# Two of the first three loads issued by GpSimd behind its first mask instead of at once, in a kernel for the diagonal of a 2-D prefix sum

## Chip, cores and metric

The kernel runs on one core of one Trainium2 chip. The metric is the time of one execution on the device, in microseconds (us), as the median of several runs.

## The reference

```python
def setup_inputs():
    B, H, W = 4, 4224, 4224
    return {"x": np.random.randn(B, H, W).astype(np.float32)}

def reference(x):
    ps = np.cumsum(np.cumsum(x, axis=1), axis=2)
    diag = np.diagonal(ps, axis1=1, axis2=2)
    return np.cumsum(diag, axis=1).astype(np.float32)
```

Of each 4224 x 4224 prefix sum only the diagonal is wanted, and its running sum. The element at row i and column j enters every diagonal entry from max(i, j) on, so all of x, 285 MB, has to be read once.

## The kernel before

GpSimd loads strips of 768 rows (128 partitions x 6 rows) and converts float32 to bf16 on the way. TensorE adds up columns with a selector matrix; DVE multiplies the diagonal block with a triangular mask and sums rows; ScalarE sums other columns. Three strip buffers rotate, so the load of strip 3 waits until strip 0 has been used. A small "head" (0.54 MB of the last rows) comes through another queue, that of SyncE.

The opening, which the change touches:

```python
    NBUF = 3
    strips = ctx.enter_context(tc.tile_pool(name="strips", bufs=NBUF))
    # ...
    ctx.enter_context(tc.manual_schedule())      # program order is kept on each engine
    # ...
    nc.sync.dma_start(out=head, in_=src_a[:, :, N - HC : N])

    def strip_tile():
        return strips.tile([P, F2, N], BF16, name="strip")

    def load_rows(o, b, r0):
        f = o.shape[1]
        nc.gpsimd.dma_start(
            out=o, in_=x[b, r0 : r0 + f * P, :].rearrange("(p f) w -> p f w", f=f))

    prefetched = []
    for i in range(NBUF):                        # the three issues
        t = strip_tile()
        load_rows(t, 0, i * F2 * P)
        prefetched.append(t)

    hs = last.tile([P, 3], FP32, name="hs")
    nc.vector.reduce_sum(out=hs[:, 0:2], in_=head, axis=AX.X)   # DVE's first work: waits for the head
    # ... sel: small memsets on DVE

    def upper_mask(f):
        um = consts.tile([P, f, f * P], BF16, name=f"um{f}")
        nc.vector.memset(um, 1.0)
        nc.gpsimd.affine_select(out=um, in_=um, ...)            # waits for DVE's memset
        return um

    um6 = upper_mask(F2)
    um3 = upper_mask(F)
    # ... um1, ident, and some 20 small constants on GpSimd and DVE
```

And the main loop, which takes the strips:

```python
        for s in range(ns):
            strip = prefetched.pop(0) if prefetched else None
            if strip is None:
                strip = strip_tile()
                load_rows(strip, b, s * F2 * P)
            add_up(strip, F2, s * F2 * P, acc6[:, s], um6, by_rows=whole and s > 0)
            # ...
```

Of the kernel before, what the change touches and what calls it, by code (L numbers as in the profile page):

```python
# [17 lines left out]
def kernel(  # L18
# [18 lines left out]
    P = 128  # L37
    F = 3
    F2 = 2 * F
# [6 lines left out]
    NBUF = 3  # L46
# [24 lines left out]
# [6 lines that stand above are left out]
            out=o, in_=x[b, r0 : r0 + f * P, :].rearrange("(p f) w -> p f w", f=f)  # L77
        )

    prefetched = []  # L80
    for i in range(NBUF):
        t = strip_tile()
        load_rows(t, 0, i * F2 * P)
        prefetched.append(t)


    hs = last.tile([P, 3], FP32, name="hs")
# [6 lines left out]
# [4 lines that stand above are left out]
        nc.gpsimd.affine_select(  # L98
            out=um,
            in_=um,  # L100
            compare_op=ALU.is_gt,
            fill=0.0,
            base=0,
            pattern=[[-1, f], [1, f * P]],
            channel_multiplier=-f,
        )
        return um
# [2 lines left out]
    nc.vector.tensor_copy(out=sel_f, in_=sel)  # L110

    um6 = upper_mask(F2)
    um3 = upper_mask(F)
    um1 = consts.tile([P, GW], BF16, name="um1")
    nc.vector.memset(um1, 1.0)
# [484 lines left out]
```

## Time and profile before

| | before |
|---|---|
| time, median of the first 3 runs | 667.52 us (667.36 to 668.04) |
| span of the profiled run | 665.9 us |
| DMA queue of the strip loads | 142.47 MB written, 99.9% of the 16 engines' span |
| DVE, PE, ACT, GpSimd busy | 57%, 31%, 20%, 5% |

The busy shares say that no compute engine is the bound, and the line of DMA shares, nines in all slices but the last, that the loads are. Such a kernel is lost or won in two places only: at its two ends, and wherever the loads might run dry. The prediction shows and reads the lines.

One more view: the chain of work that ended last. In the kernel before, its first 60 us run from the issue of strip 0 straight to that strip's landing (columns: start us, us, what):

```profile
1.33 33.81 DMA strip<-in_x_dram
...
35.16 2.57 DVE mu L356
```

### The profile page before, as it was taken

The page shows a single profiled execution, that of the slowest core. Times are in us where ns is not written, and L with a number is a line of the kernel's source. Part 1 is how long each engine was busy: PE and PEld are TensorE (multiplying, and loading weights), DVE is VectorE, ACT ScalarE, POOL GpSimd, SP SyncE. Part 2 cuts the span into 40 slices and gives each one's busy share as a digit, 9 for nine tenths or more (in the row PEclk, how much of TensorE's full clock was granted, in tenths as well). Part 3 has the DMA queues.
Part 4 walks back from the last instruction along what each step waited for, and adds up shares of the span by engine and source line. Part 5 has one row for each costly group of instructions (what it writes and reads, how often), then busy time and mean ns, then how long its engine had stood idle before and what let it go on. Part 6 is the DMA issues. An engine that isn't in the chain of part 4 may idle for free.

```text
span 665.9 us, 2495 instructions
## 1 busy us (share of the span) xinstructions
PE 205.2 (31%) x948; PEld 94.0 (14%) x948; DVE 380.9 (57%) x176; ACT 136.1 (20%) x219; POOL 31.3 (5%) x59
## 2 busy tenths in 40 slices
PE   0070522302117143140311723404031354350428
PEld 0030211100003021010100311201000131120103
DVE  4160828476946183756794526456589434362866
ACT  0000121406300103040630020304063002030434
POOL 4200000000000000000000000000000000001000
PEclk9995857656558585665655857657565595775758
DMA  9999999999999999999999999999999999999998
GB/s 203 219 219 218 219 213 213 212 218 219 219 219 218 218 220 216 218 215 212 218 219 218 218 218 219 218 216 217 215 215 218 218 216 216 218 219 218 213 210 163
DMA packets 7650, 143.23 MB, mean 215 GB/s; under 512 B 682, under 2 KB 982, under 8 KB 2134
## 3 DMA queue, kind: packets, MB, share of 16 engines
q0 software_dynamic: 7296, 142.47, 99.9%
q1 hardware_dynamic: 342, 0.61, 0.3%
q8 instruction: 7, 0.11, 0.1%
q14 instruction: 5, 0.04, 0.0%
HBM read 285.47 MB, written 0.07 MB: 429 GB/s over the span
## 4 chain that ended last, share of the span: by engine, by line
DVE 51%; another core or an unknown queue 35%; DMA 12%; PE 1%; issue 1%; POOL 0%; DVEq 0%; POOLq 0%
DVE acc L261 27%; DMA strip<-in_x_dram 12%; DVE mu L356 7%; DVE strip L357 7%; DVE rowed L261 7%; PE d L214 1%; DVE c L487 0%; DVE whole_sums L487 0%; POOL strip L452 0%; DVE pu L261 0%; DVE whole_sums L282 0%; POOL strip L441 0%; DVE acc L381 0%; DVE rows L408 0%
## 5 line engine op out<-in xcount | busy, mean ns | idle before, releaser
L256 ACT ACTIVATE dump<-strip 128x416 bf16<-128x416 bf16 (+6 forms) x108 | 124.4, 1152 | 520.5 <-DMA strip<-in_x_dram 517.8
L356 DVE TENSOR_TENSOR mu<-strip,um 128x4608 bf16<-128x4608 bf16 (+1 forms) x24 | 52.4, 2183 | 256.9 <-DMA strip<-in_x_dram 256.8
L261 DVE TENSOR_REDUCE acc<-strip 128x6 f32<-128x4608 bf16 (+6 forms) x23 | 195.9, 8517 | 0.4
L221 PEld LDWEIGHTS <-sel 128*11 128x11 bf16 x643 | 66.6, 104 | 477.8 <-issue 448.1
L214 PE MATMUL d<-strip,sel 128*11 128x384 bf16 x90 | 37.1, 412 | 296.9 <-DMA strip<-in_x_dram 296.9
L221 PE MATMUL d<-strip,sel 128*11 128x384 bf16 x441 | 115.6, 406 | 0.0
L357 DVE TENSOR_TENSOR strip<-strip,mu 128x4608 bf16<-128x4608 bf16 (+1 forms) x24 | 52.4, 2183 | 1.0
L214 PE MATMUL d<-mu,sel 128*11 128x384 bf16 x43 | 16.3, 379 | 108.5 <-DVE mu L356 108.5
L261 DVE TENSOR_REDUCE rowed<-strip 128x384 f32<-128x2304 bf16 x12 | 48.9, 4079 | 0.0
L221 PE MATMUL d<-mu,sel 128*11 128x384 bf16 x200 | 46.3, 366 | 0.0
L76 POOL DMA_DIRECT2D strip<-in_x_dram x24 | 16.5, 687 | 537.9 <-DVE acc L261 292.7
L256 ACT ACTIVATION_READ_ACCUMULATOR dump<-strip 128x1 f32 x108 | 20.1, 186 | 0.0
L214 PE MATMUL d<-rowed,sel_f 128*11 128x384 f32 x24 | 11.7, 573 | 20.7 <-DVE rowed L261 20.7
L214 PEld LDWEIGHTS <-sel 128*11 128x11 bf16 x134 | 13.6, 102 | 24.1 <-issue 12.2
L214 PE MATMUL d<-ident,rows 128*11 128x128 f32 x24 | 5.2, 379 | 16.8 <-DVE rows L417 16.8
L261 DVE TENSOR_REDUCE pu<-d 11x1 f32<-11x384 f32 x4 | 2.2, 546 | 6.2 <-PE d L214 6.2
L97 DVE MEMSET um<- 128x4608 bf16 (+1 forms) x2 | 4.9, 2458 | 1.1 <-issue 1.1
L98 POOL TENSOR_SCALAR_AFFINE_SELECT um<-um 128x4608 bf16<-128x4608 bf16 (+1 forms) x2 | 5.2, 2610 | 7.5 <-DVE um L97 7.5
L214 PE MATMUL d<-halves,rows 128*11 128x64 f32 x48 | 5.3, 289 | 0.0
L214 PEld LDWEIGHTS d<-ident,rows 128*11 128x11 f32 x24 | 2.5, 119 | 18.9 <-DVE rows L417 11.7
L214 PEld LDWEIGHTS d<-rowed,sel_f 128*11 128x11 f32 x24 | 1.4, 92 | 25.3 <-DVE rowed L261 25.0
L214 PEld LDWEIGHTS d<-halves,rows 128*11 128x11 f32 x48 | 4.8, 129 | 1.3 <-issue 1.1
(105 smaller groups left out, 60.8 us busy)
## 6 DMA issues: line engine op xcount, KB each, us to landing
strip<-in_x_dram POOLq DMA_DIRECT2D x19, 6336.0 KB, 72.7
strip<-in_x_dram POOLq DMA_DIRECT2D x5, 3168.0 KB, 55.8
strip<-in_x_dram POOLq DMA_DIRECT2D x1, 1080.0 KB, 49.9
strip<-in_x_dram POOLq DMA_DIRECT2D x1, 768.0 KB, 52.9
strip<-in_x_dram POOLq DMA_DIRECT2D x3, 256.0 KB, 54.2
head<-in_x_dram SPq DMA_DIRECT2D x1, 528.0 KB, 3.7
strip<-in_x_dram POOLq DMA_DIRECT2D x1, 192.0 KB, 43.2
strip<-in_x_dram POOLq DMA_DIRECT2D x1, 64.0 KB, 28.7
```

Source lines behind the costliest of these rows:

```text
L76: nc.gpsimd.dma_start(out=o, in_=x[b, r0 : r0 + f * P, :].rearrange("(p f) w -> p f w", f=f))
L97: nc.vector.memset(um, 1.0)
L98: nc.gpsimd.affine_select(out=um, in_=um, compare_op=ALU.is_gt, fill=0.0, base=0, pattern=[[-1, f], [1, f * P]], channel_multiplier=-f,)
L214: nc.tensor.matmul(o, lhsT=lhsT, rhs=rhs, start=start, stop=False, skip_group_check=True)
L221: te.add_instruction(mybir.InstMatmult(start_tensor_calc=False, stop_tensor_calc=False, tile_position=(0, 0), tile_size=(P, P if lhsT.shap ...
L256: nc.scalar.activation(out=dump[:, :w], in_=src, func=ACT.Copy, accum_out=acc)
L261: nc.vector.reduce_sum(out=acc, in_=src, axis=AX.X)
L356: nc.vector.tensor_mul(out=mu, in0=block, in1=um)
L357: nc.vector.tensor_sub(out=block, in0=block, in1=mu)
```

## The change

GpSimd is to issue only strip 0 at once, then make its first mask, and issue strips 1 and 2 behind it. The intent that one can read from it: the first load should not share GpSimd with the two that are not needed yet, and since strip 0 takes 30 us to arrive, the others have time.

```diff
     prefetched = []
-    for i in range(NBUF):
+
+    def prefetch():
         t = strip_tile()
-        load_rows(t, 0, i * F2 * P)
+        load_rows(t, 0, len(prefetched) * F2 * P)
         prefetched.append(t)
+
+    prefetch()
@@
     um6 = upper_mask(F2)
+    for i in range(1, NBUF):
+        prefetch()
     um3 = upper_mask(F)
```

## The prediction

> **What bounds the kernel now.** I began with the page: the clock line, the line of DMA shares, the queues and the HBM traffic.
>
> ```profile
> PEclk9995857656558585665655857657565595775758
> DMA  9999999999999999999999999999999999999998
> GB/s 203 219 219 218 219 213 213 212 218 219 219 219 218 218 220 216 218 215 212 218 219 218 218 218 219 218 216 217 215 215 218 218 216 216 218 219 218 213 210 163
> ...
> q0 software_dynamic: 7296, 142.47, 99.9%
> ...
> HBM read 285.47 MB, written 0.07 MB: 429 GB/s over the span
> ```
>
> All forty slices but the last have the DMA engines at 90% or more, and one queue (q0, the loads that GpSimd issues) owns 99.9% of it. The busiest compute engine, DVE, has 57%. So the time is that of one stream: 142.47 MB written into SBUF, twice that read from HBM because the loads turn float32 into bf16. Then I read the end of the chain of work, from 600 us on:
>
> ```profile
> 607.31 11.72 another core or an unknown queue
> 619.03 0.28 issue
> 619.32 43.23 DMA strip<-in_x_dram
> ```
>
> The last load ends at 619.32 + 43.23 = 662.55 us; what follows is 665.9 - 662.55 = 3.35 us of tail. Last, the stretches and the timeline of the opening, where the change acts (a row of stretches gives the busy time of PE, PEld, DVE, ACT and POOL, each with its instructions, then clock, DMA share and GB/s):
>
> ```profile
> 1.00:2.00 1.00, 0.00 (x0) 0.00 (x0) 0.00 (x0) 1.00 (x1) 0.67 (x1) 1.00 0.07 11
> 2.00:3.00 1.00, 0.00 (x0) 0.00 (x0) 0.00 (x0) 0.09 (x1) 1.00 (x3) 1.00 0.79 167
> ...
> 60.00:630.00 570.00, 174.86 (x786) 80.06 (x786) 336.22 (x117) 122.50 (x198) 17.58 (x27) 0.63 1.01 217
> ```
>
> ```profile
> 1.33 2.27 POOL L76 DMA_DIRECT2D strip<-in_x_dram  x3 [0.81 <-POOLq L584]
> 4.59 1.25 DVE L88 TENSOR_REDUCE hs<-head 128x2 f32<-128x1056 f32 x1 [4.59 <-DMA head<-in_x_dram]
> 7.12 3.90 DVE L97 MEMSET um<- 128x4608 bf16 x1 [0.90 <-issue]
> 11.09 4.06 POOL L98 TENSOR_SCALAR_AFFINE_SELECT um<-um 128x4608 bf16<-128x4608 bf16 x1 [7.50 <-DVE um L97]
> 12.60 0.17 DVE L127 MEMSET ident<- 128x128 f32 x1
> 17.01 0.23 DVE L140 TENSOR_TENSOR halves<-ident 128x64 f32<-128x64 f32 x1 [4.24 <-POOL ident L128]
> 21.24 0.24 POOL L203 IOTA steps<- 128x128 int32 x1
> 35.16 2.56 DVE L356 TENSOR_TENSOR mu<-strip,um 128x4608 bf16<-128x4608 bf16 x1 [11.63 <-DMA strip<-in_x_dram]
> 46.45 0.78 POOL L76 DMA_DIRECT2D strip<-in_x_dram  x1 [24.97 <-PE d L221]
> 65.17 2.56 DVE L356 TENSOR_TENSOR mu<-strip,um 128x4608 bf16<-128x4608 bf16 x1 [19.87 <-DMA strip<-in_x_dram]
> ```
>
> The reader is to see four things. GpSimd issues three strips in 2.27 us. The small head load lands at 4.59 us and starts DVE, whose memset of the first mask (ends 11.02) releases GpSimd's select (ends 15.15). Strip 0 starts the real work at 35.16 and strip 1 at 65.17, 30.0 us apart. And between 15 and 35 us only setup runs.
>
> The floor: 142.47 MB at the 217 GB/s of the 60 to 630 us stretch is 656.5 us. Everything else in the span is 665.9 - 656.5 = 9.4 us: start, tail, small irregularities.
>
> **What the Trainium skill says.** "DMA: Bandwidth & Descriptors", Specifications, gives the DMA fabric a ceiling of 435 GB/s and HBM per core about 358. The trace reads 429 GB/s over the span, and 434 in the middle (2 x 217): the stream stands at the first ceiling, and above the second, so here the measurement decides against the 358. The same page, Queues, rings and completion order, says that an engine takes its ring's descriptors in order and switches between queues at packet boundaries. The trace agrees as far as it goes: strips land in the order of issue, 30.0 us apart, though three were queued at once. "Perfetto Trace Analysis", DMA Instruction — SWDGE, says that the record of such an issue ends with descriptor generation, not with the data: here 0.76 us per issue (2.27 / 3) against some 30 us of transfer. "SBUF — State Buffer", Who interferes with whom, says that DVE in a two-port mode can lock GpSimd out; the timeline has DVE idle from 12.77 to 17.01, just where the two moved issues would go, so I expect no such block.
>
> **The change part by part.** The order of instructions of both builds differs on GpSimd alone: DVE, PE, ACT and SP keep their sequence and what they wait for. No byte of traffic is added or removed.
>
> Taken away: two issues from about 2.1 to 3.6 us. Strip 0's own issue stays first at 1.33, so the stream's start stays. What might gain is the time until strip 0's first packet. The packet records have the first strip packet at about 3.7 us, 0.1 us after the third issue ends, so perhaps strip 0 becomes visible only when GpSimd is through with all three. But the head load has the engines until then: on 15 of 16 engines the first strip packet begins within some 0.02 us of the head's last record. Gain 0 to 0.7 us, of which I take 0.2.
>
> Added: the same two issues after the first mask. GpSimd waits for DVE's memset as before, ends the select at 15.15, and issues strips 1 and 2 from 15.2 to 16.7 (2 x 0.76 = 1.5 us). Are they in time? Strip 0 keeps all engines busy until just before 35.1. From an issue to its first packet I estimate 2.4 us (1.33 to 3.7, the head included), so strip 1 is ready at about 17.6 and strip 2 at 18.4, against 35.1: a reserve of 17 us. The engines never run dry, and strip 1 still lands at 65.1.
>
> Moved: all of GpSimd's later setup by 1.5 us. The identity ends at 18.5 instead of 17.0, the last iota at 23.0 instead of 21.5; DVE's setup ends at 25.0 instead of 23.5. DVE is next needed at 35.16, after an idle 11.63 us that falls to about 10.1. GpSimd's next issue, at 46.45, came after 24.97 us of waiting for PE; that becomes 23.4 and ends at the same moment.
>
> Sum on the path that sets the end: -0.2 (start) + 0 (strip 1 in time) + 0 (setup hidden) = -0.2 us. **667.52 - 0.2 = 667.3 us.**
>
> **The rivals.** First, starvation: if something holds the mask back, strips 1 and 2 wait behind it, since GpSimd works in order. The weak link is the head load, which DVE awaits first. If strip 0's packets, visible earlier, got between the head's, the head's 16 packets on an engine would each wait for a strip packet of 1.89 us (packet records), up to 30 us. The head at 27 us instead of 4.6 moves the mask's end from 15.2 to about 37.6 and strip 1's first packet to 40: 5 us of dry engines, 672.5 us; at the full 30 us delay some 12 us, 680 us. For it: the first strip packet follows the head so closely that nothing shows what happens when they meet. Against it: the head's packets start at about 1.9 us, before strip 0's issue has ended (2.1), and when strip packets appear the other engines finish their head first. I give this 4%.
>
> Second, the earlier start as a real gain: if strip 0's visibility was held back and the engines had time to spare, the whole stream moves forward by up to 1.5 us (the two issues): 666.0 us. The records of the head speak against more than half of it. One detail leaves a door open: the first strip packet lasted 3.11 us instead of 1.89, and one engine then finished strip 0 about 0.75 us behind the other 15. If that slow packet was an accident of three issues at once, its 0.75 us comes back: 666.8 us.
>
> Third, a shallower queue: for some 13 us only one strip is queued instead of three. If the engines needed more queued work for their rate, strip 0 would land later than 35.1. Nothing in the trace shows this state, but 16 packets per engine are queued in one strip. At a loss of 5% over 13 us it would be 0.65 us: 668.2 us.
>
> **Range and chances.** The three runs of before lie within 667.36 and 668.04, and another chip or session may shift that by 0.1 to 0.2%, or about 1 us. With gains of up to 1.5 us and small losses I set 665.8 to 669.0 us. Faster by over 2% means 13.4 us saved, more than the 9.4 us that exist beside the stream: practically excluded, 0.003. Slower by over 2% needs strip 1's first packet 13.4 us after 35.1, hence an issue no earlier than about 46 us: possible only with nearly the worst form of the first rival, 0.012.
>
> **What would show it.** In the changed kernel's timeline: the head's reduce still at 4.6 us, the select ending at 15.2, two issues at 15.2 to 16.7, DVE's setup ending at about 25.0, its first strip at 34.5 to 35.2 and the second 30.0 us later, GpSimd's fourth strip near 46.4 with a wait of about 23.4 us for PE, and the DMA line still all 9s. A second strip more than 30.5 us behind the first would prove starvation; a head after 5 us would name its cause; a first strip before 34.5 would prove the second rival. The prediction is wrong if the engines run dry at 35 us, or if the stream's rate in mid-kernel leaves 217 GB/s.

## The result, and the profile after

The changed kernel took 667.78 us (median of 6 runs, 667.38 to 669.75), the kernel before 667.75 us in its six runs (667.19 to 669.69). The ratio is 1.0001, with a 95% interval of 0.9983 to 1.0018: the same. (A ratio is the mean time of one kernel's runs over the mean time of the other's in the same rounds, so it is not quite the ratio of the medians.) Over all sessions the changed kernel had 17 runs with a mean of 668.53 us and the kernel before 43 runs with a mean of 668.56 us.

The timeline of the opening of the changed kernel (start us, us, engine, line, operation, names, shapes, and in brackets the idle time before it and what ended it):

```profile
1.33 0.82 POOL L76 DMA_DIRECT2D strip<-in_x_dram  x1 [0.81 <-POOLq L589]
...
4.56 1.25 DVE L91 TENSOR_REDUCE hs<-head 128x2 f32<-128x1056 f32 x1 [4.56 <-DMA head<-in_x_dram]
...
11.06 4.06 POOL L101 TENSOR_SCALAR_AFFINE_SELECT um<-um 128x4608 bf16<-128x4608 bf16 x1 [8.91 <-DVE um L100]
...
15.07 1.46 POOL L76 DMA_DIRECT2D strip<-in_x_dram  x2
...
18.43 0.23 DVE L145 TENSOR_TENSOR halves<-ident 128x64 f32<-128x64 f32 x1 [5.70 <-POOL ident L133]
...
22.67 0.24 POOL L208 IOTA steps<- 128x128 int32 x1
...
34.50 2.56 DVE L361 TENSOR_TENSOR mu<-strip,um 128x4608 bf16<-128x4608 bf16 x1 [9.55 <-DMA strip<-in_x_dram]
...
45.17 0.76 POOL L76 DMA_DIRECT2D strip<-in_x_dram  x1 [22.27 <-PE d L226]
...
64.48 2.56 DVE L361 TENSOR_TENSOR mu<-strip,um 128x4608 bf16<-128x4608 bf16 x1 [19.85 <-DMA strip<-in_x_dram]
```

The two issues now stand at 15.07. Everything that GpSimd does after them comes 1.4 us later (the identity's reader on DVE 18.43 instead of 17.01), and the waits shrink in exchange: DVE waited 9.55 us for strip 0 instead of 11.63, GpSimd 22.27 us for PE instead of 24.97. Strip 1 follows strip 0 by 64.48 - 34.50 = 29.98 us, as before (30.01).

The page of the changed kernel, its DMA shares and its HBM traffic:

```profile
DMA  9999999999999999999999999999999999999998
...
HBM read 285.47 MB, written 0.07 MB: 429 GB/s over the span
```

Same stream, same rate. Now the chain of work that ended last, in its first 60 us:

```profile
0.82 3.72 DMA head<-in_x_dram
...
7.08 3.91 DVE um L100
...
11.06 4.01 POOL um L101
15.07 49.32 DMA strip<-in_x_dram
```

This is a trap for the reader. The chain now leads through the head, DVE's memset and the mask to the issue of strip 1, as if the mask held up the kernel. But the 49.32 us of that step run from issue to landing, and the transfer itself takes 30. The remaining 19 us strip 1 lay queued behind strip 0. A chain that follows each wait back to its issue does not know of the queue; whether the issue is critical has to be asked of the chip, and the first experiments do that.

### The profile page after: what moved, and what is told of

The parts are those of the page before. It is cut to its first block, busy times and chain, and to the rows that moved or that the text cites. A ratio compares the mean times of both kernels' runs of the same rounds, so it can differ in the third digit from the quotient of the medians.

```text
span 665.7 us, 2495 instructions
## 1 busy us (share of the span) xinstructions
PE 201.5 (30%) x948; PEld 92.7 (14%) x948; DVE 380.9 (57%) x176; ACT 136.1 (20%) x219; POOL 31.3 (5%) x59
## 4 chain that ended last, share of the span: by engine, by line
DVE 50%; another core or an unknown queue 32%; DMA 14%; POOL 1%; issue 1%; PE 1%; DVEq 0%; POOLq 0%
DVE acc L266 26%; DMA strip<-in_x_dram 14%; DVE rowed L266 7%; DVE mu L361 7%; DVE strip L362 7%; PE d L219 1%; POOL um L101 1%; DVE um L100 1%; DMA head<-in_x_dram 1%; DVE c L492 0%; DVE whole_sums L492 0%; POOL strip L457 0%; DVE pu L266 0%; DVE whole_sums L287 0%
## 5 line engine op out<-in xcount | busy, mean ns | idle before, releaser
L226 PEld LDWEIGHTS <-sel 128*11 128x11 bf16 x643 | 65.4, 102 | 475.7 <-issue 444.7
L219 PE MATMUL d<-strip,sel 128*11 128x384 bf16 x90 | 36.5, 406 | 296.5 <-DMA strip<-in_x_dram 296.5
L226 PE MATMUL d<-strip,sel 128*11 128x384 bf16 x441 | 113.3, 399 | 0.0
L219 PEld LDWEIGHTS <-sel 128*11 128x11 bf16 x134 | 13.2, 99 | 24.6 <-issue 12.6
```

The costliest lines, as they stand in the source:

```text
L219: nc.tensor.matmul(o, lhsT=lhsT, rhs=rhs, start=start, stop=False, skip_group_check=True)
L226: te.add_instruction(mybir.InstMatmult(start_tensor_calc=False, stop_tensor_calc=False, tile_position=(0, 0), tile_size=(P, P if lhsT.shap ...
```

## The experiments

Ten runs were made: six edited kernels and four unedited copies. All give correct results. Two theories stood against each other on each part:

- **The theory of the reserve**: engines that have strip 0 to move until 34 us don't care whether strip 1 is issued at 2 or at 15 us, and would not care until about 32 us.
- **The rivals**: a gain from an earlier start; a cost of the shallower queue; and the head, on whose landing strips 1 and 2 now depend.

### Later still, but in time: e1_behind_setup

Edit, against the changed kernel:

```diff
     um6 = upper_mask(F2)
-    for i in range(1, NBUF):
-        prefetch()
@@
     nc.gpsimd.iota(steps, pattern=[[4, P]], base=7, channel_multiplier=-1)
+    for i in range(1, NBUF):
+        prefetch()
```

> Strips 1 and 2 issued behind all of GpSimd's setup, at about 21.5 and 22.2 us instead of 15.1 and 15.8. Theory of the reserve: strip 0 occupies the engines until about 34 us, so 6.4 us more of delay cost nothing: 667.5 us, DVE's second strip still 30.0 us after its first. Rival (a shallow queue costs rate, or each us of delay costs something): up to 6 us more, 670 to 674 us.

Measured: 669.74 us (669.80, 667.52, 669.73, 669.76); the kernel before in the same session 667.97 us; ratio 1.0018 (1.0002 to 1.0034). The timeline:

```profile
21.45 1.50 POOL L76 DMA_DIRECT2D strip<-in_x_dram  x2
...
37.01 2.56 DVE L361 TENSOR_TENSOR mu<-strip,um 128x4608 bf16<-128x4608 bf16 x1 [13.23 <-DMA strip<-in_x_dram]
...
66.98 2.56 DVE L361 TENSOR_TENSOR mu<-strip,um 128x4608 bf16<-128x4608 bf16 x1 [19.83 <-DMA strip<-in_x_dram]
```

The issue comes 6.4 us later than in the changed kernel, and strip 1 still follows strip 0 by 29.97 us: nothing ran dry. The times alone don't settle it: the median lies just below the rival's 670 to 674 us, and the interval just excludes 1. The trace does. The 1.8 us in the medians are already there when strip 0 lands (37.01 instead of 34.50), and the records of the DMA packets show that they were lost before the moved issue at 21.45: the first 48 strip packets, over by about 12 us, took 0.8 us longer per engine, on average, than in the profile of the changed kernel. The changed kernel itself, in the same session, shows the same (next run), and one of the four runs is at 667.52. So no cost of the delay is seen, but the session had a second level of time, which the repetitions had to explain.

### The same kernels again: after_again, before_again, after_third, before_third

No edit. The first pair belonged to the sessions of the other experiments, on two chips; the second pair ran in one session on a third chip.

> The changed kernel once more, unedited, five rounds. Theory (the stream of loads is the bound and is never dry): 667.5 us, within 0.2% of the kernel before; strip 1 starts on the engines when strip 0 ends, at about 34 us. Rival (the earlier start is a real gain of up to 0.7 us): ratio 0.999 or lower with an interval that excludes 1.

> The kernel before, unedited, to see what repeats. Theory that the slow first strip packet (3.11 us) of its first profile is chance: it need not come again, and DVE's first strip starts anywhere from 34.4 to 35.2 us. Rival (three issues at once cause it): again one first packet of about 3 us and a first strip at 35.1 us. Time 667.5 us, ratio 1.000 either way.

> The changed kernel again, beside an unedited copy of the kernel before in the same call, because its repetition gave a ratio of 1.002 that just excludes 1 where the first six runs gave 1.0001. If that 0.2% belongs to the change: every copy of it is at 669.4 us, the copy of the kernel before at 667.5 to 668. If it belongs to the load of a program or the moment (the opening's packets slow or not): both kernels fall at 667.5 or at 669.5, without regard to which of the two it is.

> An unedited copy of the kernel before, in the same call. If the 0.2% belongs to the change: 667.5 to 668 us. If not: it can be at 669.5 us as the first repetition of this kernel was (669.17 us), and DVE's first strip then starts after 36 us instead of at 34.5 to 35.2.

Measured:

| run | median us | its runs | before in its session | ratio (95%) |
|---|---|---|---|---|
| after_again | 669.37 | 669.02 to 669.71 | 667.97 | 1.0020 (1.0007 to 1.0034) |
| before_again | 669.17 | 668.02 to 669.88 | 669.05 | 1.0003 (0.9984 to 1.0021) |
| after_third | 667.83 | 667.44 to 669.83 | 668.77 | 0.9990 (0.9973 to 1.0007) |
| before_third | 668.95 | 667.40 to 669.73 | 668.77 | 1.0000 (0.9982 to 1.0018) |

Taken alone, after_again would say that the change costs 0.2%. The other three take that back: unedited copies of the kernel before reach 669.2 and 669.0 us as well, and after_third, again the changed kernel, is back at 667.8. Where the slower level loses its time is seen in the packet records of the profiled runs (times in us from the start of the span, worked out from the trace):

```
profiled run    its time   first strip packet   last record of strip 0
before          667.64     3.73                 34.83
after           667.40     3.79                 34.17
before_third    667.40     3.56                 34.23
after_third     667.60     3.69                 34.93
after_again     669.37     3.50                 36.14
before_again    669.88     3.77                 36.74
e1_behind_setup 669.80     3.58                 36.68
```

In the last three, those of the slower level, many of the first packets of the engines take 2.0 to 3.2 us instead of 1.89: over the first 48 packets the excess is 0.62, 0.40 and 0.78 us per engine, against 0.03 to 0.11 in the other four. One to three engines also began strip 0 late (two of after_again at 5.16 and 5.20 us, while the last of the 16 in the profile called after began at 4.18). At the end of strip 0 the slowest of the 16 engines is 1.2 to 2.6 us behind that of the other four. That is about what is missing at the end. DVE's first strip, expected at 34.4 to 35.2 us in before_again, began at 37.07. The cause of this slow opening was not found; the kernel's order of issue is not it, since both kernels show both levels. A difference of 0.2% between the two kernels can therefore not be resolved here, in either direction, and none is claimed.

### Too late, a little: e2_behind_landing

```diff
     nc.gpsimd.iota(steps, pattern=[[4, P]], base=7, channel_multiplier=-1)
+    probe = consts.tile([P, 2], BF16, name="probe")
+    nc.gpsimd.tensor_copy(out=probe, in_=prefetched[0][:, 0, 0:2])
+    for i in range(1, NBUF):
+        prefetch()
```

(and the two issues behind the mask removed). The copy reads strip 0, so GpSimd must wait for its landing.

> Strips 1 and 2 issued only when strip 0 has landed (a 128x2 copy by GpSimd from strip 0 stands before them), at about 34.6 us. Theory: now the engines do run dry, from 34.1 us to strip 1's first packet, which by the estimate of 2.4 us from issue to first packet comes at 37.0: dry for about 3 us, and all of it is on the end: 670.5 us (669.5 to 671.5), DVE's second strip about 33 us after its first. Rival (the queue has slack elsewhere that absorbs it): 667.5 us in spite of the gap.

Measured: 673.47 us, outside the expected 669.5 to 671.5; ratio 1.0087 (1.0073 to 1.0102). Lost are 5.5 us between the medians and 5.8 by the ratio of the means, which one run of 675.3 us raises, where 3 were expected. The timeline:

```profile
34.76 2.56 DVE L363 TENSOR_TENSOR mu<-strip,um 128x4608 bf16<-128x4608 bf16 x1 [11.22 <-DMA strip<-in_x_dram]
...
34.79 2.58 POOL L208 COPY probe<-strip 128x2 bf16<-128x2 bf16 x1 [13.29 <-DMA strip<-in_x_dram]
...
37.31 1.50 POOL L76 DMA_DIRECT2D strip<-in_x_dram  x2
...
70.48 2.56 DVE L363 TENSOR_TENSOR mu<-strip,um 128x4608 bf16<-128x4608 bf16 x1 [25.50 <-DMA strip<-in_x_dram]
```

The direction is the theory's, and the size tells more. First, the copy of two elements per partition took 2.58 us: as long as the DVE instruction that started 0.03 us before it. The Trainium skill, "SBUF — State Buffer", Who interferes with whom, says that a DVE instruction with two SBUF inputs contends with a GpSimd instruction that reads SBUF, and that whichever comes first keeps the shared ports for its whole instruction. The trace agrees, with DVE's end at 37.32 and GpSimd's at 37.37; a like copy in the next run, made while DVE did nothing, took 0.19 us. So the issue came at 37.31, not at 34.6. Second, the packet records have the last record of strip 0 at 34.44 and the first packet of strip 1 at 38.81: 1.50 us after the start of the issue, not the 2.4 I had estimated, and 4.4 us dry. Third, the stream restarts slowly: 14 of the 16 engines' first packets took 2.4 to 3.1 us instead of 1.89. Strip 1 ended 35.65 us after strip 0 instead of 29.9. These 5.75 us, 4.4 dry and some 1.4 of slow restart, agree with the loss in the time.

### Too late, by much: e3_behind_compute

```diff
+            if b == 0 and s == 0:
+                probe = consts.tile([P, F2], FP32, name="probe")
+                nc.gpsimd.tensor_copy(out=probe, in_=acc6[:, 0, :, 1])
+                for i in range(1, NBUF):
+                    prefetch()
```

(placed behind the summing of strip 0, in the main loop; the issues behind the mask removed, and the row of a strip counted by a counter of its own).

> Strips 1 and 2 issued only when DVE has summed strip 0, at about 44.9 us. Theory: dry from 34.1 to about 47 us, 13 us, all of it on the end: 680.5 us (679 to 682), DVE's second strip about 43 us after its first. Rival (the buffers catch up later): clearly under 675 us.

Measured: 681.49 us, ratio 1.020 (1.0186 to 1.0214).

```profile
34.46 2.56 DVE L360 TENSOR_TENSOR mu<-strip,um 128x4608 bf16<-128x4608 bf16 x1 [10.86 <-DMA strip<-in_x_dram]
...
44.79 1.50 POOL L76 DMA_DIRECT2D strip<-in_x_dram  x2
...
77.96 2.56 DVE L360 TENSOR_TENSOR mu<-strip,um 128x4608 bf16<-128x4608 bf16 x1 [33.37 <-DMA strip<-in_x_dram]
```

DVE's first strip began at 34.46, its second 43.50 us later instead of 30.0: 13.5 us, and 13.5 us is what the medians differ by (681.49 - 667.97). This stream gave nothing back later. The engines stood dry from 34.15 to 46.29, 12.1 us; the slow restart is again the other 1.4. Together, e1 to e3 show the reserve from both sides: an issue at 21.45 is free, one at 37.31 costs 5.75 us by the trace, one at 44.79 costs 13.5. From the 1.50 us to the first packet and the end of strip 0 at about 34.1, the last free moment is an estimate of 34.1 - 1.5 = 32.6 us. The changed kernel, at 15.07, is 17.5 us away from it.

### The head behind strip 0: e4_head_late_after and e5_head_late_before

Now the dependence that the change brings in. In e4 the changed kernel gets its head load behind the issue of strip 0; a memset of one column of the head, which the load then overwrites, holds it back.

```diff
-    nc.sync.dma_start(out=head, in_=src_a[:, :, N - HC : N])
@@
     prefetch()
+    nc.gpsimd.memset(head[:, :, 0:1], 0.0)
+    nc.sync.dma_start(out=head, in_=src_a[:, :, N - HC : N])
```

e5 is the kernel before with the same two lines behind its three issues.

> The changed kernel with the head load issued behind strip 0's issue (a GpSimd memset of one column of the head, after that issue, holds it back to about 2.5 us). Rival 1 of the prediction (head and strip packets alternate): the head lands at 25 to 35 us, the mask is done at about 36 to 46, strips 1 and 2 are issued after it, and the engines run dry for 4 to 14 us: 671 to 681 us. If instead the head overtakes or shares freely: head at 5 to 7 us, mask at 16 to 18, time 667.5 us. Also: with one issue and no head in front, the first strip packet shows the true latency of an issue; under 3.2 us from the start of the span means that three issues at once held it back, 3.7 us that they did not.

> The kernel before with the head load behind its three issues, at about 4 us. If packets alternate, the head lands at 25 to 40 us as in the run before this, and DVE works strip 0 up to 15 us late, but all three strips are queued already and nothing runs dry: 667.5 us. That against 671 to 681 us of the changed kernel would show that the change ties the loads to the head. If the head shares freely: 667.5 us with the head at 6 to 8 us. First strip packet: 3.7 us if the three issues hold it back, earlier if not.

Measured: e4 683.15 us, ratio 1.0214 (1.0198 to 1.0229); e5 668.99 us, ratio 1.0002 (0.9987 to 1.0017). The kernel before had 669.05 us beside these runs, on the same chip. So e4 is 2 us over the top of the range expected for it, and e5 equals the kernel before, as expected. First e4's chain of work:

```profile
2.30 33.90 DMA head<-in_x_dram
...
36.30 1.25 DVE hs L92
...
42.80 4.01 POOL um L102
46.81 33.17 DMA strip<-in_x_dram
```

The head, issued at 2.30, needed 33.90 us instead of 3.7. The packet records show why: on each engine one head record of 2 KB alternates with one strip record, one turn taking 1.97 us (1.885 + 0.1), from the first at 7.16 us until strip 0 has no more packets; the last head record ends at 35.8. DVE waits for the head first, so the mask is done at 46.8, and only then does GpSimd issue strips 1 and 2. Here the chain is right: between 36 and 48 us the DMA engines moved nothing (fields as in the stretches of before; the last two are DMA share and GB/s):

```profile
36.00:48.00 12.00, 10.23 (x52) 5.14 (x53) 6.96 (x8) 0.00 (x0) 5.20 (x3) 1.00 0.00 0
```

In e5 the head was even later, and the mask too:

```profile
39.99 1.25 DVE L90 TENSOR_REDUCE hs<-head 128x2 f32<-128x1056 f32 x1 [39.99 <-DMA head<-in_x_dram]
...
69.52 0.77 POOL L75 DMA_DIRECT2D strip<-in_x_dram  x1 [12.63 <-issue]
```

DVE began strip 0 at 58.85 us, more than 20 us late, and strip 3 was issued at 69.52 instead of 46.45. It cost nothing, since strips 1 and 2 had been queued from the start and kept the engines supplied until about 95 us. So the same accident, a late head, costs 14 us in one order of issue and nothing in the other. This is what the change really does: it moves no time today, but makes the loads depend on the head and on DVE's order.

These two runs also settle the rival of the earlier start. With no head in front, the first strip packet came at 2.86 us in e4 (one issue) and at 2.86 us in e5 (three issues). What was expected for e4 would have read this number, taken alone, as proof that three issues hold strip 0 back; e5 refutes that. Two more issues do not delay strip 0's first packet; what is different at 3.5 to 3.8 us is the head in front. Nor did the earlier packet help: strip 0's last record was at 35.7 and 35.6 us, against 34.2 to 34.9 in the four faster profiles above. In e4 and e5 head records lay between the strip's, and 15 and 16 of the 16 first packets took over 2.0 us.

### The late head, but a mask that does not wait for it: e6_head_late_mask_first

e4 plus one moved line: DVE's sum of the head comes behind the memsets of the masks.

```diff
-    nc.vector.reduce_sum(out=hs[:, 0:2], in_=head, axis=AX.X)
@@
     um1 = consts.tile([P, GW], BF16, name="um1")
     nc.vector.memset(um1, 1.0)
+    nc.vector.reduce_sum(out=hs[:, 0:2], in_=head, axis=AX.X)
```

> The changed kernel with the late head, but with DVE's sum of the head moved behind the memsets of the masks, so that the mask no longer waits for the head. If the cost of the late head is only DVE's order: the select ends at about 10 us, strips 1 and 2 are issued at 10 to 11.5, and the time is back at 667.5 us though the head still lands late. Rival (the late head costs the stream itself, by its packets between the strip's): the time stays with the run with the late head.

Measured: 668.75 us, ratio 1.0001 (0.9983 to 1.0019).

```profile
6.18 4.06 POOL L101 TENSOR_SCALAR_AFFINE_SELECT um<-um 128x4608 bf16<-128x4608 bf16 x1 [3.91 <-DVE um L100]
...
10.19 1.46 POOL L75 DMA_DIRECT2D strip<-in_x_dram  x2
...
37.99 1.25 DVE L121 TENSOR_REDUCE hs<-head 128x2 f32<-128x1056 f32 x1 [30.27 <-DMA head<-in_x_dram]
```

The head still lands at 38 us, the issues stand at 10.19, and the whole 14 us of e4 are gone. The late head in itself did not cost the stream those 14 us; the order in which DVE and GpSimd waited for it did. No version is faster than the two kernels: the stream of 656 us is the same in all.

## Why the prediction was right, point by point

- **The bound.** Right. DMA shares and the HBM rate of 429 GB/s are unchanged, and e3 shows that time added to the stream comes out at the end in full (13.5 of 13.5 us). Two readings of the Trainium skill beside it don't hold as I put them, and the sum needs neither. "DMA: Bandwidth & Descriptors", Specifications, gives 435 GB/s as the ceiling of SBUF's DMA ports; into SBUF this stream writes 217 GB/s, and only its rate on the HBM side, 434 (2 x 217), is near that figure, so that the stream stands at this ceiling is not shown. And the measurement does not decide against the 358 GB/s: the same page, Bandwidth, says that this is each core's part when both cores of an HBM domain stream, and here the program had one core.
- **The start, -0.2 us.** The profiled pair happens to show it (spans 665.9 and 665.7), but it is not shown to be an effect: either kernel varies by 2 us. The reason I gave for a gain, that three issues may hold strip 0 back, is refuted by e4 and e5 (2.86 us in both). The slow first packet of 3.11 us that I noticed is not tied to three issues either: e4, with one issue, has first packets of up to 3.2 us, and before_third, with three, none above 2.2.
- **Strip 1 in time.** Right: issues at 15.07 (predicted 15.2), strips 29.98 us apart. The reserve was put at 17 us and comes out at 17.5, by luck: two errors of about 1 us cancel. The engines run out of strip 0 at about 34.1 and not 35.1 us, and an issue takes 1.50 us to its first packet and not 2.4, which had included the head's packets.
- **The setup moved by 1.5 us.** Right (1.4 measured): 18.43 and 22.91 (22.67 + 0.24), hidden in DVE's wait of 9.55 us (about 10.1 predicted) and in GpSimd's wait of 22.27 us (23.4 predicted; strip 0 landed 0.66 us earlier in that run, and PE released the buffer 10.67 us after DVE's start on it instead of 11.29).
- **First rival, the late head.** Its mechanism is real, and e4 shows it: packets of the two queues alternate. It was rightly given a small chance: in the change as made, the head's packets begin at 1.9 us and strip 0's could at 2.86 (from e4), and the engines finish the head first. The worst case that I worked out, 680 us, was a little low; e4 had 683.15 us, since the head came at 36.3 us and the stream restarted slowly.
- **Third rival, a shallow queue.** No sign of it: a single queued strip ran at 1.89 us per packet in the opening, like three, and in e1, with one strip queued, the 16 engines moved 219 GB/s from 10 to 21 us.
- **The range.** It was set on runs of one session. The medians of 667.78 and 667.83 us lie in it, but the median of after_again, 669.37 us, does not: the two levels of time that both kernels have were not in the three runs I had seen, and I allowed 1 us for what turned out to be 2.

## What to carry to other kernels

Where one stream of loads is the bound, ask of each issue only whether it comes before the queue runs dry; before that moment its place was free here, after it every microsecond counted in full, and each of the three times that the stream ran dry (e2, e3, e4) its slow restart cost some 1.4 us more. Don't take a chain of waits for proof, as it counts time in the queue as time of the transfer. And before a load is put behind other work, look at everything that this work waits for: here a small load on another queue, harmless for the time, decides whether the big stream continues.

## What the Trainium skill lacked or had wrong

- No page that I read says which side of a load that converts its type counts against the ceiling of 435 GB/s in "DMA: Bandwidth & Descriptors". Here 429 GB/s were read from HBM over the span, and 217 written into SBUF in mid-kernel. The runs show both rates, and not which of them is the limit.
- The same page, Queues, rings and completion order, has the engines switch between queues at packet boundaries, but gives no consequence for a small load beside a large one. In e4 a load of 0.54 MB took 33.90 us instead of 3.7, as each of its 2 KB records waited for one strip record of 1.89 us. That a head which came first was finished first, without alternation (first strip packets at 3.5 to 3.8 us although 2.86 is possible), it doesn't explain; the runs leave it open too.
- No page that I read has the slow restart of engines that ran dry (in e2, 14 of 16 first packets at 2.4 to 3.1 us instead of 1.89; in e4 and e5, with no head in front, the opening itself began so), nor the two levels of time, 2 us apart, that unedited copies of one kernel showed.
